# Stacked half blocks in neighbourhood attention, linear attention in smaller steps, and raw weight transfers issued later

## The chip, the cores and the metric

The kernel runs on one core of a Trainium2 chip. Its time is the device time of one execution, in microseconds. The core has TensorE (matrix products, written to eight PSUM banks), VectorE, ScalarE (ACT) and GpSimd (POOL) for the rest, and SyncE (SP), whose queue issues nearly all transfers. Every engine works through its own list of instructions in order, and they meet at semaphores.

## The reference, cut to what matters

One inference step of a two-layer model of width 2048, on 128 context tokens and 512 latent tokens (640 columns in all):

```
per layer:  h = rms_norm(x) * (1 + scale) + shift          # from a conditioning vector
            y = mixer(h @ w_in) * silu(gate);  x = x + g * (y @ w_out)
layer 1:    windowed attention (8 heads)  ||  gated linear attention (4 heads, both directions)
layer 2:    neighbourhood attention (8 heads)  ||  chunked spatial gating

gla_scan, per chunk:   att = tril(qi @ ki.T)
                       o   = att @ v + qi @ S
                       S   = exp(blast) * S + ks.T @ v

neighbourhood_attention: 64 columns x 8 rows of latent tokens; each query sees 8 rows x 16 columns
                       of keys near it and all 128 context keys; softmax; o = p @ v
```

All numbers are float32. Projections are done to nearly float32 precision with three fast products: a weight w is split into whi (rounded) and wlo (the remainder), an activation into acth and actl, and acth*whi + actl*whi + acth*wlo is summed.

## The kernel before, in words

**The stream of projections.** A chunk is 128 output columns of a projection. `units` goes through the 16 k-tiles of a chunk in quads and through two halves of 320 (or 322) tokens; each k-tile and half is three matmuls. Raw weights come into `wraws`, four buffers of 512 columns that rotate (`wslot`, `wneed`); ACT makes whi and POOL wlo (`wpump`), into rings with room for five quads (`whl`). A raw load goes out when the split that read its buffer is done.

**Other work between the projections.** Attention, linear attention and the modulation sums are Python generators (tasks). While the program is written, `Pace` keeps a clock for every engine, for SP and for the transfers, from cost formulas; `self.now` is TensorE's. After every few projection matmuls `tick` lets tasks write their next step, up to the next `yield`. `until(x)` yields until the planner believes x ready; `bank()` yields until the next small PSUM bank is believed free. So the planner decides only where an instruction stands in its engine's list; on the chip the engine then waits for what is not really there. `dma` puts a transfer into SP's list at once if its buffer is believed ready, else into `late`, from which `dmas` issues it when it is.

**Banks.** In the first layer three banks are for the projections (`npj` is 3) and three (`top` is 6) rotate for everything small (`sm`); two hold rows of the modulation. From the end of the first layer's attention `npj` is 5.

**Linear attention** (`gla_pe`, one run a head): transposes of the decayed keys `KS` of both directions, local products (`At`), states (`p`), then the outputs `outs` for chunks (0, 1), (2) and (3, 4), with a state update on VectorE (`next_state`) in between. State updates read the banks that `states` filled and write two buffers in turn, which `outs` reads. The values have been transposed just before by `tok_major` (four blocks in a bank, the fifth in the next).

**Windowed attention** (`even_head`): after the scores, one group of matmuls in one bank, with 512 columns for the context and then 256, 384, 384 and 256 for the four key blocks, all of 128 rows. `rope` first turns the queries, with four transfers within SBUF and work on VectorE and POOL.

**Neighbourhood attention** (`na_head`): keys are taken in five blocks, the first and the last of 64 tokens, the three between of 128. Values (`vk`) and probabilities (`pT`) are transposed block by block. The output group is one 512-column matmul for the context, one of 128 columns on 64 rows, three of 256 columns on 128 rows and one of 128 columns on 64 rows. `open_na` lays out the buffers.

In the profile L400 is the one line at which all matmuls are issued, L405 the one for transposes, L436 that for transfers, L215 that for everything on ACT, VectorE and POOL. "Y" and "arena" are large areas from which many buffers are cut.

## Time and profile before

| | us |
|---|---|
| median of 3 runs | 2090.88 (2089.56 to 2090.99) |
| the profiled execution's own time | 2094.82 |
| its span in the profile | 2093.0 |
| TensorE busy | 2047.3 |
| VectorE, POOL, ACT busy | 1327.3, 1275.1, 1064.4 |

In rows of the view in order of time, the first number is the start, the second how long the row's instructions take together, then engine, line, operation, what it writes and reads, shape, and how many (x); in brackets how long the engine was idle before, and who ended that. A row of waits has the total, the number and the longest. TensorE's ends are modelled, so the steady rate is read from starts. A plain float32 matmul leaves two records, a transpose one. In rows by stretch come the stretch, its length, busy time of TensorE, of weight loads, of VectorE, ACT and POOL with instruction counts, the granted clock, and the transfers' share and rate.

### The profile page before, as it was taken

To read this page: it belongs to the slowest core of one execution; us is meant where nothing else is said; L and a number is where in the kernel's file an instruction comes from. 1 tells how busy PE (TensorE), PEld (TensorE's weight loads), DVE (VectorE), ACT (ScalarE), POOL (GpSimd) and SP (SyncE) were. 2 spreads that over 40 slices of the span, in tenths; PEclk is the share of its full clock that TensorE was granted. 3 is DMA by queue.
4 is the path that set the end of the run, shared out by engine and by line. 5 is a ranking of instruction groups with operands and counts; after the bars stand their busy time and mean duration, and the time that the engine had idled before them with its cause. 6 is when DMAs were issued, how large, how long until landed. Compare 5 with 4: busy or idle time off the path is not lost. (4 is left out here: it accounts for less than half of the span.)

```text
span 2093.0 us, 40200 instructions
## 1 busy us (share of the span) xinstructions
PE 2047.3 (98%) x14345; PEld 1995.9 (95%) x14345; DVE 1327.3 (63%) x3070; ACT 1064.4 (51%) x2446; POOL 1275.1 (61%) x1072
## 2 busy tenths in 40 slices
PE   7999999999999999999999999999999999999997
PEld 6889999999999999999999999999999999999997
DVE  4757677676555655788786878787454554456444
ACT  5545555445665765444564434444444554454443
POOL 4655454445545554788765666655555577768884
PEclk9999999999999999999999999999999999999998
DMA  9956333436456444577734454454322334363427
GB/s 367 396 195 205 124 122 110 142 112 188 153 170 190 142 137 148 167 222 226 249 131 135 136 159 153 139 156 139 98 86 95 95 129 135 112 235 121 139 90 251
DMA packets 192697, 340.18 MB, mean 163 GB/s; under 512 B 20752, under 2 KB 70000, under 8 KB 192496
## 3 DMA queue, kind: packets, MB, share of 16 engines
q1 hardware_dynamic: 191296, 336.45, 49.7%
q8 instruction: 112, 1.84, 0.4%
q10 hardware_dynamic: 1200, 1.17, 0.2%
q14 instruction: 89, 0.73, 0.1%
HBM read 303.03 MB, written 31.88 MB: 160 GB/s over the span
## 5 line engine op out<-in xcount | busy, mean ns | idle before, releaser
L400 PE MATMUL bank<-acth,whi 128*128 128x320 f32 (+3 forms) x3320 | 1017.7, 317 | 4.7 <-ACT YB L215 1.4
L400 PE MATMUL bank<-acth,wlo 128*128 128x320 f32 (+3 forms) x3320 | 991.7, 310 | 0.9 <-POOL wlo L215 0.9
L400 PE MATMUL bank<-actl,whi 128*128 128x320 f32 (+3 forms) x3320 | 991.5, 310 | 0.0
L215 POOL TENSOR_TENSOR wlo<-wraw,whi 128x512 fp32r<-128x512 f32 (+1 forms) x446 | 568.1, 1285 | 439.1 <-ACT whi L215 368.4
L400 PEld LDWEIGHTS bank<-acth,whi 128*128 128x128 f32 (+1 forms) x3320 | 614.9, 188 | 12.5 <-issue 3.0
L400 PEld LDWEIGHTS bank<-actl,whi 128*128 128x128 f32 (+1 forms) x3320 | 615.5, 188 | 1.7
L400 PEld LDWEIGHTS bank<-acth,wlo 128*128 128x128 f32 (+1 forms) x3320 | 614.1, 188 | 1.9 <-POOL wlo L215 1.9
L215 POOL TENSOR_TENSOR wlo<-rs,whi 128x384 fp32r<-128x384 f32 x370 | 407.9, 1120 | 205.6 <-ACT whi L215 173.2
L215 ACT ACTIVATE whi<-wraw 128x512 fp32r<-128x512 f32 (+1 forms) x456 | 261.3, 588 | 126.7 <-PE bank L400 85.7
L215 ACT ACTIVATE whi<-rs 128x384 fp32r<-128x384 f32 x370 | 184.4, 518 | 83.2 <-PE bank L400 69.1
L400 PE MATMUL bank<-eh,whi 128*128 128x322 f32 (+1 forms) x666 | 208.9, 314 | 1.0 <-ACT whi L215 1.0
L400 PE MATMUL bank<-eh,wlo 128*128 128x322 f32 (+1 forms) x666 | 206.8, 310 | 1.2 <-POOL wlo L215 0.9
L400 PE MATMUL bank<-el,whi 128*128 128x322 f32 (+1 forms) x666 | 206.3, 310 | 0.0
L215 DVE CUSTOM_DVE_ANT_0 adas<-adas,bank,partg 128x256 bf16<-128x256 f32 (+1 forms) x296 | 160.6, 543 | 15.6 <-DMA adas<-ada_g 8.0
L215 DVE TENSOR_TENSOR wraw<-rs 128x768 f32<-128x768 f32 x74 | 98.8, 1335 | 100.7 <-DMA rs<-w_odd 55.4
L215 POOL TENSOR_TENSOR prod<-adas,mixrow 128x512 f32<-128x512 f32 x76 | 99.4, 1317 | 68.5 <-ACT prod L215 47.9
L215 ACT ACTIVATE arena<-arena,bc 128x512 f32<-128x512 f32 (+4 forms) x189 | 97.8, 538 | 78.6 <-DVE arena L215 73.7
L400 PEld LDWEIGHTS bank<-eh,wlo 128*128 128x128 f32 x666 | 125.1, 188 | 2.4 <-POOL wlo L215 2.4
L400 PEld LDWEIGHTS bank<-eh,whi 128*128 128x128 f32 x666 | 125.4, 188 | 1.3 <-ACT whi L215 1.2
L400 PEld LDWEIGHTS bank<-el,whi 128*128 128x128 f32 x666 | 125.4, 188 | 0.0
L215 DVE CUSTOM_DVE_ANT_0 adas<-adas,bank,part 128x512 bf16<-128x512 f32 x150 | 111.6, 744 | 19.6 <-DMA adas<-ada 16.7
L215 DVE TENSOR_TENSOR bank<-bank,sums 128x320 f32<-128x320 f32 (+1 forms) x148 | 70.8, 493 | 82.5 <-PE bank L400 61.3
(226 smaller groups left out, 2458.9 us busy)
## 6 DMA issues: line engine op xcount, KB each, us to landing
wraw<-w_even SPq DMA_DIRECT2D x176, 256.0 KB, 3.4
adas<-ada_g SPq DMA_DIRECT2D x128, 256.0 KB, 3.7
adas<-ada SPq DMA_DIRECT2D x128, 256.0 KB, 3.7
rs<-w_odd SPq DMA_DIRECT2D x50, 384.0 KB, 3.3
wraw<-w_odd SPq DMA_DIRECT2D x74, 256.0 KB, 3.6
wraw<-w_out SPq DMA_DIRECT2D x60, 256.0 KB, 3.9
rs<-w_odd SPq DMA_DIRECT2D x50, 256.0 KB, 3.8
Y<-ada SPq DMA_DIRECT2D x24, 512.0 KB, 7.8
```

Of the source, the lines that this page charges most:

```text
L215: return f(*args, **kw)
L400: self.nc.tensor.matmul(out, lhsT, rhs, start=start, stop=stop, **kw)
```

## The change

Four things are edited.

1. `dma`: while `npj` is 3, a transfer into `wraws` is put into SP's list 2.0 us of the planner's clock after its buffer is believed ready.
2. `gla_pe`: the transposes of the keys are written in three steps instead of two (four of one direction, the two last blocks, four of the other); steps wait with `bank()` for a free bank, and some start 0.5 or 0.6 us later.
3. `na_head`: the first and last 64-token blocks share one 128-row block. In `vk` the last block's values go to rows 64 to 127 beside the first block's in rows 0 to 63. In `pT` the two have their own 128 columns and zeros in the other 64 rows (two memsets in `open_na`). One matmul with 256 moving columns then writes the first and the fourth quarter of the bank. The last block is transposed with the 64 tokens before it, so that it comes out in rows 64 to 127.
4. `na_head`: where two probability blocks lie side by side, one copy of 256 columns takes the place of two.

```
-        if pc.ready("q", o, i) <= self.now + 0.1:
+        lag = 2.0 if self.npj == 3 and out.name.rstrip("0123456789_").startswith("wraw") else 0.0
+        if pc.ready("q", o, i) + lag <= self.now + 0.1:
             emit()
         else:
-            pc.late.append((emit, o + i, lambda: pc.ready("q", o, i)))
+            pc.late.append((emit, o + i, lambda: pc.ready("q", o, i) + lag))
...
-        yield from self.until(KS[0], KS[1])
-        pb = self.sm()
+        yield from self.until(KS[1])
+        yield 0.6
+        yield from self.bank()
         pa = self.sm()
         for i in range(4):
             self.tr(pa[:, c(i)], KS[1][:, c(i)])
+        nc.scalar.activation(KS[1][:, 0:512], pa, AF.Copy)
+        yield from self.until(KS[0])
+        yield 0.6
+        yield from self.bank()
+        pb = self.sm()
         self.tr(pb[:, 0:128], KS[1][:, c(4)])
         self.tr(pb[:, 128:256], KS[0][:, c(4)])
-        nc.scalar.activation(KS[1][:, 0:512], pa, AF.Copy)
         nc.scalar.activation(KS[1][:, 512:640], pb[:, 0:128], AF.Copy)
         nc.scalar.activation(KS[0][:, 512:640], pb[:, 128:256], AF.Copy)
-        yield
+        yield 0.6
+        yield from self.bank()
...
         yield from self.until(At, Sb)
+        yield 0.5
+        yield from self.bank()
         outs((0, 1), (None, S))
         S3 = next_state(S2, 2)
         yield from self.until(S2)
+        yield from self.bank()
         outs((2,), (S2,))
         S4 = next_state(S3, 3)
         yield from self.until(S4)
+        yield 0.5
+        yield from self.bank()
         outs((3, 4), (S3, S4))
...
-        for i, t in ((0, 0), (1, 4)):
-            a, e = edges[t]
-            self.tr(pv[:64, 128 * i : 128 * i + 128], vl[:, a:e])
-        nc.scalar.activation(vk[:64, 512:768], pv[:64, 0:256], AF.Copy)
+        self.tr(pv[:64, 0:128], vl[:, 0:64])
+        self.tr(pv[:, 128:256], vl[:, 384:512])
+        nc.scalar.activation(vk[:64, 512:640], pv[:64, 0:128], AF.Copy)
+        nc.scalar.activation(vk[64:, 512:640], pv[64:, 128:256], AF.Copy)
...
+            if b in (1, 2):
+                s = slot[(b, b)]
+                nc.vector.tensor_copy(pT[:, s : s + 256], pt[:, 128:384])
...
-        self.mm(po[:, 0:128], vkt[0], pT[:64, 768:896], start=False, stop=False)
         for j in (1, 2, 3):
...
-        self.mm(po[:, 384:512], vkt[4], pT[:64, 896:1024], start=False, stop=True)
+        ends = po.rearrange("p (a b) -> p a b", b=128)[:, 0:4:3, :]
+        self.mm(ends, vk[:, 512:640], pT[:, 768:1024].rearrange("p (a b) -> p a b", b=128), start=False, stop=True)
...
+            nc.gpsimd.memset(L["pT"][64:, 768:896], 0.0)
+            nc.gpsimd.memset(L["pT"][:64, 896:1024], 0.0)
```

What this does to the order of instructions is shown at three places. First, TensorE at the key transposes of the linear attention's first head. Banks 68 and 69 are projections, 70 to 72 the three small ones; "ident" marks a transpose, the arena holds the values and one direction's keys, Y the other's. Before:

```order
L400 MATMUL bank_69<-acth,wlo 128x320
L405 MATMUL bank_71<-ident,arena_1639 128x128 x4
L405 MATMUL bank_72<-ident,arena_1639 128x128
L405 MATMUL bank_71<-ident,arena_1639 128x128 x4
L405 MATMUL bank_70<-ident,arena_1639 128x128
L405 MATMUL bank_70<-ident,Y 128x128
```

and now:

```order
L405 MATMUL bank_71<-ident,arena_1639 128x128 x4
L405 MATMUL bank_72<-ident,arena_1639 128x128
L400 MATMUL bank_69<-acth,whi 128x320
L400 MATMUL bank_69<-actl,whi 128x320
L400 MATMUL bank_69<-acth,wlo 128x320
...
L405 MATMUL bank_70<-ident,arena_1639 128x128 x4
...
L405 MATMUL bank_71<-ident,arena_1639 128x128
L405 MATMUL bank_71<-ident,Y 128x128
```

The values' transposes (the first two rows of transposes) were followed at once by the keys', back into bank 71. Now six projection matmuls stand between, the keys' four go to bank 70, and after six more the last two go to bank 71.

Second, TensorE at the same head's outputs. Before:

```order
L400 MATMUL bank_71<-Y,arena_1639 128x128 x8
L400 MATMUL bank_72<-Y,arena_1639 128x128 x6
L400 MATMUL bank_69<-acth,whi 128x320
L400 MATMUL bank_69<-actl,whi 128x320
L400 MATMUL bank_69<-acth,wlo 128x320
...
L400 MATMUL bank_70<-Y,arena_1639 128x128 x12
```

and now:

```order
L400 MATMUL bank_71<-Y,arena_1639 128x128 x8
L400 MATMUL bank_69<-acth,whi 128x320
L400 MATMUL bank_69<-actl,whi 128x320
L400 MATMUL bank_69<-acth,wlo 128x320
...
L400 MATMUL bank_72<-Y,arena_1639 128x128 x6
L400 MATMUL bank_67<-acth,whi 128x322
L400 MATMUL bank_67<-actl,whi 128x322
L400 MATMUL bank_67<-acth,wlo 128x322
...
L400 MATMUL bank_70<-Y,arena_1639 128x128 x12
```

The outputs of chunks 0 and 1 (x8) and of chunk 2 (x6) stood together; now six projection matmuls lie between them, and twelve, where there were six, before the last (x12).

Third, SP's list ahead of the first query head's rotary transfers in windowed attention ("Y<-arena", four transfers of 32 rows). Before:

```order
L436 DMA adas<-ada 128x512 x3
L436 DMA wraw<-w_even 128x512
L436 DMA adas<-ada 128x512 x2
L436 DMA Y<-arena_4740 32x512 x3
L436 DMA adas<-ada 128x512
L436 DMA Y<-arena_4740 32x512
```

and now:

```order
L436 DMA adas<-ada 128x512
L436 DMA wraw<-w_even 128x512
L436 DMA adas<-ada 128x512 x3
L436 DMA wraw<-w_even 128x512
L436 DMA Y<-arena_4744 32x512 x3
L436 DMA adas<-ada 128x512
L436 DMA Y<-arena_4744 32x512
```

Raw loads ("wraw") stand further back among the modulation loads ("adas"); here one has come to stand directly ahead of the rotary transfers.

## The prediction

> **What bounds the kernel now.** I read the page's busy times first, then busy time by stretches, then TensorE's own waits stage by stage, and last the order in time at the places that the change touches.

> ```profile
> span 2093.0 us, 40200 instructions
> PE 2047.3 (98%) x14345; PEld 1995.9 (95%) x14345; DVE 1327.3 (63%) x3070; ACT 1064.4 (51%) x2446; POOL 1275.1 (61%) x1072
> 200.00:300.00 100.00, 97.19 (x663) 94.62 (x662) 75.36 (x131) 54.77 (x109) 48.34 (x33) 1.00 0.38 116
> 1550.00:1650.00 100.00, 100.00 (x669) 96.76 (x668) 43.09 (x114) 47.85 (x119) 57.41 (x53) 1.00 0.31 99
> ```

> TensorE (first number after the stretch's length) is busy for 98% of the span, and no other engine comes near. What counts is therefore only what TensorE does and what makes it stand still. The linear attention of the first layer (200 to 470 us) leaves it idle for some us; the neighbourhood attention of the second layer (1350 to 1700 us) leaves it nothing, so there only shorter matrix work can help. The granted clock is 1.00 in both rows.

> The waits of TensorE, first from 145 to 840 us, then from 215 to 470 us alone:

> ```profile
> PE bank L405 <- ACT arena L215: 5.2, 8, 1.8
> PE bank L400 <- DVE arena L215: 4.0, 5, 2.2
> PE bank L405 <- DVE sh L215: 1.1, 1, 1.1
> PE bank L400 <- ACT bc L215: 0.6, 1, 0.6
> ...
> PE bank L405 <- ACT arena L215: 3.1, 6, 0.6
> PE bank L400 <- DVE arena L215: 1.8, 4, 0.8
> ```

> Ten waits lie in the linear attention, 4.9 us as the view counts them. No row names whi or wlo, the split weights: from 145 to 840 us TensorE never stood waiting for a weight.

> **Linear attention, the transposes.** The last of the four heads on TensorE, and ACT beside it:

> ```profile
> 444.43 0.32 PE L400 MATMUL bank<-acth,wlo 128*128 128x322 f32 x1
> 444.58 0.71 PE L405 MATMUL bank<-ident,arena 128*128 128x128 f32 x5
> 445.87 0.77 PE L405 MATMUL bank<-ident,arena 128*128 128x128 f32 x5 [0.58 <-ACT arena L215]
> ...
> 445.22 0.77 ACT L215 ACTIVATE arena<-bank 128x512 f32<-128x512 f32 x2 [0.47 <-PE bank L405]
> ```

> The row ahead is the last projection matmul: what follows it starts 0.15 us later, and so does each projection in a run of them. Five transposes of the values are followed at once by five of the keys. The first four of both go to the same bank (the order shown with the change has it), so the second group waits until ACT has copied that bank out, from 445.22 on. A transpose in an unbroken row takes 0.108 us (worked out below). Five are 0.54, and the next group starts after 445.87 - 444.58 = 1.29, not 0.54. The view's 0.58 starts only at the modelled end of the last transpose, which overlaps the next start when nothing waits, so the path loses the whole difference, 0.75. Taken for the four heads this is 4 x 0.75 = 3.0 us. The change puts the keys' four in the third bank, six projection matmuls later. What hides the copy is then 6 x 0.15 = 0.9 us of projections. Without them, the third bank would still be free of that copy.

> **Linear attention, the outputs.** Heads one and four on TensorE, then VectorE in head four:

> ```profile
> 236.97 1.95 PE L400 MATMUL bank<-Y,arena 128*128 128x128 f32 x16
> 239.70 1.60 PE L400 MATMUL bank<-Y,arena 128*128 128x128 f32 x12 [0.78 <-DVE arena L215]
> ...
> 458.90 1.95 PE L400 MATMUL bank<-Y,arena 128*128 128x128 f32 x16
> 461.20 1.60 PE L400 MATMUL bank<-Y,arena 128*128 128x128 f32 x12 [0.35 <-DVE arena L215]
> ...
> 460.67 0.48 DVE L215 SCALAR_TENSOR_TENSOR arena<-arena,etot,bank 128x256 f32<-128x256 f32 x1 [2.16 <-PE bank L400]
> ```

> Here TensorE hands to VectorE and back: the state update at 460.67 waits for the first outputs and takes 0.48, and the next outputs wait for it. Sixteen records at 0.112 take 1.79 us; the next group starts after 2.30 in head four and after 2.73 in head one. That loses 0.51 and 0.94, and the other two heads show 0.35 like head four. Together 0.94 + 3 x 0.51 = 2.5 us. The change asks for a free bank before the second group, and at least six projections (0.9 us) come between. They cover 0.51 entirely and 0.94 nearly; if VectorE is busy with something else, up to the old 2.5 us comes back.

> Do more and smaller pieces cost anything by themselves? Four transposes between projections:

> ```profile
> 225.52 0.60 PE L405 MATMUL bank<-ident,Y 128*128 128x128 f32 x4
> 225.87 0.39 PE L400 MATMUL bank<-acth,whi 128*128 128x322 f32 x1
> 226.10 0.31 PE L400 MATMUL bank<-actl,whi 128*128 128x322 f32 x1
> ```

> From 225.52 to the second projection, 0.58; less one projection (0.15) that is 0.43, four transposes at 0.108. Changing over costs nothing that can be seen, so three more pieces a head are free. Of 3.0 + 2.5 I take off 0.1 for head one, whose 0.94 is more than the cover, and put **-5.4 us** on the linear attention. Its bounds are 0, if each wait comes back elsewhere, and -6.3 us, if the two waits that are left (3.1 us of ACT waits in six rows, less 4 x 0.58, is 0.8) go too.

> **Half blocks.** A head's last group of matmuls in neighbourhood attention, with the first projections behind it; then the same kind of group in the first layer's windowed attention, where every block has 128 rows; then durations by form, and the weight loads of the first group:

> ```profile
> 1357.03 3.34 PE L400 MATMUL bank<-Y 128*128 128x512 f32 x12
> 1360.30 0.41 PE L400 MATMUL bank<-acth,whi 128*128 128x320 f32 x1
> 1360.55 0.31 PE L400 MATMUL bank<-actl,whi 128*128 128x320 f32 x1
> ...
> 806.08 3.17 PE L400 MATMUL bank<-arena 128*128 128x512 f32 x10
> 808.90 0.50 PE L400 MATMUL bank<-acth,whi 128*128 128x320 f32 x1
> 809.24 0.31 PE L400 MATMUL bank<-actl,whi 128*128 128x320 f32 x1
> ...
> L400 PE MATMUL bank<-Y 64*128 64x128 f32 x32 | 7.8, 322 | 0.0
> L400 PE MATMUL bank<-Y 128*128 128x128 f32 x16 | 3.1, 275 | 0.0
> ...
> 1357.98 1.58 PEld L400 LDWEIGHTS bank<-Y 64*128 64x128 f32 x8 [0.76 <-issue]
> ```

> Each plain f32 matmul leaves two records. The windowed group has 512 + 256 + 384 + 384 + 256 = 1792 columns, 3584 in its ten records; from 806.08 to 809.24 less one projection of 0.15 is 3.01 us, 0.84 ns a column. The neighbourhood group has 512 + 128 + 3 x 256 + 128 = 1536 columns, 3072 in twelve records: at 0.84 they should take 2.58. They take 1360.55 - 1357.03 - 0.15 = 3.37. The 0.79 too much belongs to the two half blocks: their weight loads start only after the matmuls before them are through (0.76 of idle ahead of the first), where full blocks load behind running matmuls, and each of their records is longer than a full one of the same width (322 against 275 ns). The change has the same 1536 columns with 128 rows everywhere, so 2.58 us a head. TensorE is never idle in that stage, nothing else can take the place of the bound, and 8 x 0.79 = **-6.3 us** follow.

> [...]

> What no row shows is a matmul that writes two separate quarters of a bank. It lies between a full 256-column matmul (2 x 0.216 at 0.84 ns a column) and the pair it replaces (that plus 0.79). I take the first, because nothing but the view of the bank differs.

> The rest of this edit is off the path. VectorE has two copies fewer a head (two of 128 columns become one of 256, twice), ACT one more of 64 rows by 128 columns. Transposing 128 instead of 64 columns does not show in these rows, nor does the memset, twice 64x128 once:

> ```profile
> L405 PE MATMUL bank<-ident,Y 128*128 128x128 f32 x82 | 15.9, 273 | 0.0
> L405 PE MATMUL bank<-ident,Y 128*64 128x128 f32 x15 | 4.1, 272 | 0.0
> L215 ACT ACTIVATE Y<-bank 64x256 f32<-64x256 f32 x7 | 2.6, 367 | 0.0
> L215 POOL MEMSET part<- 128x64 f32 x1 | 0.2, 151 | 0.0
> ```

> ACT gains below 0.37 us a head at 48% busy; POOL gets at most 2 x 0.2 us, with weight remainders behind it. Uncovered, either would be under 3 us.

> **The held transfers.** A raw load now goes out 2.0 us (by the planner's clock) after its buffer is free, behind the modulation loads issued meanwhile. Transfers to landing, POOL's splits and the SP queue's waits:

> ```profile
> wraw<-w_even SPq DMA_DIRECT2D x176, 256.0 KB, 3.4
> L215 POOL TENSOR_TENSOR wlo<-wraw,whi x155: 1007/1293/2446, 144.3 to 833.6; 128x512 fp32r<-128x512 f32 x154, 128x384 fp32r<-128x384 f32 x1
> SPq L436 <- POOL wlo L215: 204.5, 92, 9.0
> ```

> 155 splits in 689 us are one in 4.4 us, and four buffers rotate, so a buffer is read again about 17.8 us after its last split. Less 1.3 for the split and 3.4 for landing, about 13 us are spare; 2.0 of them cost nothing. SP stood 204.5 us for POOL between 145 and 640 us; some of that goes, and what is queued behind (modulation, state and rotary transfers) may start earlier. TensorE waited for none of them but one:

> ```profile
> 543.16 1.83 DVE L215 TENSOR_TENSOR arena<-arena 128x512 f32<-128x512 f32 x1 [4.48 <-DMA Y<-arena]
> 546.71 0.49 PE L400 MATMUL bank<-arena 128*128 128x128 f32 x2 [2.15 <-DVE arena L215]
> ```

> This is windowed attention's first head, waiting for the rotary step on VectorE, which had waited for its transfers. In the new order its scores stand six projections earlier (138 instead of 144 behind the value head's transposes), while the query's own place is the same. So this wait should grow by 6 x 0.15: **+0.9 us**, between -2.2 (wait gone) and +3 (a raw load now stands directly ahead of the rotary transfers).

> **The sum.** -5.4 - 6.3 + 0.9 = -10.8 us on the profiled execution's own 2094.8 us, 2084.0. That execution stands 3.9 us above the median of 2090.88, so the median should come to **2080.1 us**.

> **The rivals.**
> (a) The hold frees the SP queue more than I count: the rotary wait (2.15) and the two left-over ACT waits (0.8) go. Then 2080.1 - 0.9 - 2.2 - 0.8 = 2076.2. For it: 204.5 us of SP waiting. Against: most of what SP carries is not waited for by TensorE.
> (b) The linear attention's waits only move, to the next bank or the next state: 2080.1 + 5.4 = 2085.5. For it: three banks in rotation and VectorE 70% busy there. Against: 0.9 us of projections at each place.
> (c) Row count does not matter and the half blocks give nothing: 2080.1 + 6.3 = 2086.4. Against: 0.79 us of surplus beside a group of full blocks.
> (d) Slower: the hold reaches the path at the four raw buffers. It decides once bursts of splits eat the 13 us; each load that misses its turn costs TensorE up to 2.0 us. One load in ten of the 155, 15 or 16, would be 31 us, 2111; it takes eight for 2096. Against: not one wait for a weight before.

> **How the numbers follow.** My forecast 0.57, (a) 0.14, (b) 0.17, (c) 0.04, (d) 0.03, and 0.05 for changes of order in windowed attention that I cannot price. What this kernel's measurement can tell from no change is 0.2%, 4.2 us, so below 2086.7 is faster. The first three cases are 0.88, with half of (c) and a little of the rest: 0.91 faster, 0.06 same, 0.03 slower. The range runs from 2075.0, a little under (a), to 2086.0, a little over (b).

> **What would show it.** In the changed profile no record of a 64-row matmul, the neighbourhood group at 2.6 us instead of 3.4, no 0.58 wait for ACT among the keys' transposes, no wait for VectorE between the outputs, still no wait for whi or wlo, and about 3 us at the first rotary wait. I am wrong if the neighbourhood group stays over 3 us, if a new row of waits of a few us stands in the linear attention, or if whi or wlo shows up among TensorE's waits before 840 us.

## The result, and the profile after

| | before | changed |
|---|---|---|
| median of 12 runs | 2090.03 us | 2084.37 us |
| lowest and highest | 2086.29 and 2097.17 | 2080.28 and 2089.64 |
| the profiled execution's own time | 2094.82 | 2084.71 |

The ratio is 0.9969, with a 95% interval of 0.9959 to 0.9978: the change makes the kernel about 6 us faster. The forecast was 2080.1 us, 10.8 less than before. The sign came as forecast and the time lies inside the range (2075.0 to 2086.0), but little more than half of the gain arrived. The profiled executions lie 10.1 us apart, which looks like the forecast's sum. It isn't: the one of before stood 4.8 us over the median of its kernel, the one of the change 0.3. So what follows reads pieces out of the profiles, and takes totals from repeated runs.

The page of the changed kernel, its first lines:

```profile
span 2082.9 us, 40154 instructions
PE 2042.3 (98%) x14329; PEld 1999.2 (96%) x14329; DVE 1329.2 (64%) x3048; ACT 1070.5 (51%) x2460; POOL 1276.9 (61%) x1077
```

TensorE is the bound as before. In neighbourhood attention, the last matmul group of a head and the projections behind it, in order of time:

```profile
1352.43 2.75 PE L400 MATMUL bank<-Y 128*128 128x512 f32 x10
1354.83 0.50 PE L400 MATMUL bank<-acth,whi 128*128 128x320 f32 x1
1355.16 0.31 PE L400 MATMUL bank<-actl,whi 128*128 128x320 f32 x1
```

From 1352.43 to 1355.16, less one projection of 0.15, is 2.58 us: what the prediction gave for 1536 columns at 0.84 ns, to the hundredth. The groups by form, from 1300 to 1760 us, of the changed kernel (busy time, mean ns of one, idle time before):

```profile
L400 PE MATMUL bank<-Y 128*128 128x256 f32 x64 | 15.1, 379 | 0.0
L400 PEld LDWEIGHTS bank<-Y 128*128 128x128 f32 x88 | 15.9, 190 | 5.1 <-issue 3.8
```

and of the kernel before, where the records of 64 rows stood beside those of 128:

```profile
L400 PE MATMUL bank<-Y 128*128 128x256 f32 x48 | 12.5, 396 | 0.0
L400 PEld LDWEIGHTS bank<-Y 128*128 128x128 f32 x72 | 12.2, 189 | 1.8
L400 PEld LDWEIGHTS bank<-Y 64*128 64x128 f32 x32 | 4.7, 184 | 8.7 <-issue 7.4 <-DVE partg L215 0.7 <-DVE arena L215 0.3
```

The form with 64 rows is gone, and with it the 8.7 us of idle time ahead of its weight loads. The loads of 128 rows now stand idle for 5.1 us instead of 1.8, so of 10.5 us in all, 5.4 are saved. The 16 new records (two for each of eight heads) that write two separate quarters of a bank are among the 64, and these take 379 ns on average, not more than the 396 of the 48 before; the group as a whole runs at the 0.84 ns a column of a group without such a view. So the strided output shows no cost.

In the linear attention, TensorE's waits from 215 to 470 us, and then the fourth head's value and key transposes and its first two output groups:

```profile
PE bank L400 <- DVE Y L215: 0.9, 1, 0.9
PE bank L400 <- ACT bc L215: 0.7, 1, 0.7
PE bank L405 <- ACT arena L215: 0.7, 2, 0.4
```

```profile
441.24 0.71 PE L405 MATMUL bank<-ident,arena 128*128 128x128 f32 x5
442.67 0.60 PE L405 MATMUL bank<-ident,arena 128*128 128x128 f32 x4
...
457.40 1.95 PE L400 MATMUL bank<-Y,arena 128*128 128x128 f32 x16
460.07 1.50 PE L400 MATMUL bank<-Y,arena 128*128 128x128 f32 x12
```

The 0.58 ahead of the key transposes and the 0.35 ahead of the second outputs (445.87 and 461.20 before) are gone: projections stand in between now, and neither row has a wait. Of the ten old waits, 4.9 us, two are left with 0.7 us. But two new ones have come that the kernel before had nowhere in this stretch:

```profile
294.25 0.41 PE L400 MATMUL bank<-acth,whi 128*128 128x320 f32 x1 [0.75 <-ACT bc L215]
...
342.81 0.41 PE L400 MATMUL bank<-r,wgs 96*128 96x320 f32 x1 [0.92 <-DVE Y L215]
```

By who ends these waits, both are for work that ACT and VectorE have not finished yet. Together they take 1.67 us.

Then comes windowed attention. In order of time around 510 us, VectorE, ACT and TensorE, and the place at 845 us:

```profile
505.63 3.48 DVE L215 TENSOR_TENSOR Y<-Y,arena 128x512 f32<-128x512 f32 x2 [2.44 <-DMA arena<-Y]
509.03 0.73 DVE L215 CUSTOM_DVE_ANT_0 adas<-adas,bank,partg 128x512 bf16<-128x512 f32 x1
...
512.98 0.75 DVE L215 CUSTOM_DVE_ANT_0 adas<-adas,bank,partg 128x512 bf16<-128x512 f32 x1
513.65 0.49 DVE L215 TENSOR_TENSOR arena<-bank,rstd 128x320 f32<-128x320 f32 x1
514.17 0.17 ACT L215 ACTIVATE bc<-bank 128x2 f32<-128x2 f32 x1 [2.63 <-DVE arena L215]
514.39 0.41 PE L400 MATMUL bank<-acth,whi 128*128 128x320 f32 x1 [2.08 <-ACT bc L215]
...
844.91 0.72 PE L400 MATMUL bank<-acth,whi 128*128 128x320 f32 x2 [1.96 <-ACT eh L215]
```

This is read backwards. TensorE waits for ACT, ACT for VectorE's copy at 513.65, and VectorE works in order: ahead of that copy stand six modulation sums (adas), ahead of them the rotary step of a key head, and that had waited 2.44 us for its transfers within SBUF. The same place before, with five sums between the first two rows:

```profile
509.69 3.47 DVE L215 TENSOR_TENSOR Y<-Y,arena 128x512 f32<-128x512 f32 x2 [3.09 <-DMA adas<-ada_g]
...
516.91 0.49 DVE L215 TENSOR_TENSOR arena<-bank,rstd 128x320 f32<-128x320 f32 x1
...
517.65 0.41 PE L400 MATMUL bank<-acth,whi 128*128 128x320 f32 x1 [0.55 <-ACT bc L215]
```

There the rotary step had waited no less (3.09 us), and TensorE stood for 0.55 us only. Counted from the start of the rotary step, VectorE's copy now begins after 8.02 us instead of 7.22, and TensorE's wait after 6.68 instead of 7.41; these two make up the 1.53 us by which the wait has grown. By stretches:

```profile
200.00:300.00 100.00, 98.42 (x677) 96.08 (x675) 79.53 (x133) 55.35 (x110) 50.20 (x34) 1.00 0.38 119
...
500.00:600.00 100.00, 95.62 (x618) 91.40 (x617) 58.19 (x160) 58.76 (x162) 54.03 (x41) 0.97 0.52 170
515.05:521.88 6.83, 6.14 (x25) 5.68 (x24) 4.93 (x13) 5.76 (x14) 4.88 (x5) 0.50 0.76 243
800.00:900.00 100.00, 97.23 (x638) 95.19 (x637) 70.23 (x139) 48.53 (x103) 67.42 (x52) 0.98 0.56 178
```

The granted clock, the third number from the end, is 1.00 in the linear attention. After the wait of 2.08 us it is 0.50 for 6.83 us, after that of 1.96 for 3.41 us. Projections then start 0.268 us apart instead of 0.147, so 3.41 us at 0.50 lose about 1.5 us. The kernel before had 0.50 nowhere between 100 and 2060 us of its profile.

The raw loads, waits of SP's queue from 145 to 640 us, in the changed kernel:

```profile
SPq L436 <- POOL wlo L215: 156.7, 66, 9.8
```

It was 204.5 us in 92 waits. And from 145 to 840 us no wait of TensorE names whi or wlo.

### The profile page after: what moved, and what is told of

Same layout as the page of the kernel before. It is cut to its first block, busy times and chain, and to the rows that moved or that the text cites. A ratio compares the mean times of both kernels' runs of the same rounds, so it can differ in the third digit from the quotient of the medians.

```text
span 2082.9 us, 40154 instructions
## 1 busy us (share of the span) xinstructions
PE 2042.3 (98%) x14329; PEld 1999.2 (96%) x14329; DVE 1329.2 (64%) x3048; ACT 1070.5 (51%) x2460; POOL 1276.9 (61%) x1077
## 5 line engine op out<-in xcount | busy, mean ns | idle before, releaser
L400 PE MATMUL bank<-acth,whi 128*128 128x320 f32 (+3 forms) x3320 | 1021.5, 319 | 8.6 <-ACT bc L215 2.8
L400 PE MATMUL bank<-acth,wlo 128*128 128x320 f32 (+3 forms) x3320 | 993.2, 310 | 0.9 <-POOL wlo L215 0.8
L400 PE MATMUL bank<-actl,whi 128*128 128x320 f32 (+3 forms) x3320 | 993.3, 310 | 0.0
L215 POOL TENSOR_TENSOR wlo<-wraw,whi 128x512 fp32r<-128x512 f32 (+1 forms) x446 | 566.1, 1282 | 450.9 <-ACT whi L215 374.0
L400 PEld LDWEIGHTS bank<-acth,whi 128*128 128x128 f32 (+1 forms) x3320 | 616.4, 188 | 16.8 <-ACT bc L215 4.8
L400 PEld LDWEIGHTS bank<-actl,whi 128*128 128x128 f32 (+1 forms) x3320 | 617.1, 189 | 1.9
L400 PEld LDWEIGHTS bank<-acth,wlo 128*128 128x128 f32 (+1 forms) x3320 | 615.8, 188 | 1.5 <-POOL wlo L215 1.4
L215 POOL TENSOR_TENSOR wlo<-rs,whi 128x384 fp32r<-128x384 f32 x370 | 406.3, 1117 | 189.5 <-ACT whi L215 156.0
L215 ACT ACTIVATE whi<-wraw 128x512 fp32r<-128x512 f32 (+1 forms) x456 | 261.6, 589 | 126.3 <-PE bank L400 82.9
L215 ACT ACTIVATE whi<-rs 128x384 fp32r<-128x384 f32 x370 | 184.2, 519 | 77.3 <-PE bank L400 62.3
L400 PE MATMUL bank<-eh,whi 128*128 128x322 f32 (+1 forms) x666 | 208.7, 313 | 0.0
L400 PE MATMUL bank<-eh,wlo 128*128 128x322 f32 (+1 forms) x666 | 206.4, 310 | 0.2 <-POOL wlo L215 0.2
L400 PE MATMUL bank<-el,whi 128*128 128x322 f32 (+1 forms) x666 | 206.3, 310 | 0.0
L215 DVE CUSTOM_DVE_ANT_0 adas<-adas,bank,partg 128x256 bf16<-128x256 f32 (+1 forms) x296 | 160.8, 543 | 14.0 <-DMA adas<-ada_g 5.4
L215 DVE TENSOR_TENSOR wraw<-rs 128x768 f32<-128x768 f32 x74 | 96.8, 1308 | 97.9 <-DMA rs<-w_odd 40.9
L215 POOL TENSOR_TENSOR prod<-adas,mixrow 128x512 f32<-128x512 f32 x79 | 101.8, 1299 | 62.2 <-ACT prod L215 49.4
L215 ACT ACTIVATE arena<-arena,bc 128x512 f32<-128x512 f32 (+4 forms) x189 | 98.0, 540 | 74.3 <-DVE arena L215 69.4
L400 PEld LDWEIGHTS bank<-eh,wlo 128*128 128x128 f32 x666 | 125.1, 188 | 0.5 <-POOL wlo L215 0.5
L400 PEld LDWEIGHTS bank<-eh,whi 128*128 128x128 f32 x666 | 125.4, 188 | 0.1
L400 PEld LDWEIGHTS bank<-el,whi 128*128 128x128 f32 x666 | 125.3, 188 | 0.0
L215 DVE TENSOR_TENSOR bank<-bank,sums 128x320 f32<-128x320 f32 (+1 forms) x148 | 70.7, 493 | 84.2 <-PE bank L400 63.1
L215 DVE CUSTOM_DVE_ANT_0 adas<-adas,bank,part 128x512 bf16<-128x512 f32 x147 | 109.4, 744 | 16.4 <-DMA adas<-ada 13.6
## 6 DMA issues: line engine op xcount, KB each, us to landing
wraw<-w_even SPq DMA_DIRECT2D x176, 256.0 KB, 3.7
adas<-ada_g SPq DMA_DIRECT2D x128, 256.0 KB, 3.6
adas<-ada SPq DMA_DIRECT2D x128, 256.0 KB, 3.6
wraw<-w_odd SPq DMA_DIRECT2D x74, 256.0 KB, 3.6
wraw<-w_out SPq DMA_DIRECT2D x60, 256.0 KB, 3.8
rs<-w_odd SPq DMA_DIRECT2D x50, 256.0 KB, 3.9
```

The lines of the kernel that those rows point to most:

```text
L215: return f(*args, **kw)
L400: self.nc.tensor.matmul(out, lhsT, rhs, start=start, stop=stop, **kw)
```

## The experiments

The theory was: each part does in its place about what the prediction's rows say, and part of it is lost later, where a wait of nearly 2 us in windowed attention or at the handover behind it lowers the clock. Its rivals: one part is simply worth less than forecast; the hold costs more than its 0.9 us; the lowered clock belongs to something else than waits.

### Each part alone, and the change without the hold

First the half blocks and the joint copies alone (edits 3 and 4):

```
-        self.mm(po[:, 0:128], vkt[0], pT[:64, 768:896], start=False, stop=False)
...
-        self.mm(po[:, 384:512], vkt[4], pT[:64, 896:1024], start=False, stop=True)
+        ends = po.rearrange("p (a b) -> p a b", b=128)[:, 0:4:3, :]
+        self.mm(ends, vk[:, 512:640], pT[:, 768:1024].rearrange("p (a b) -> p a b", b=128), start=False, stop=True)
...
```

> Only the stacked half blocks (edits 3 and 4), the rest as before. Theory A (my sum: half blocks -6.3, linear attention -5.4, hold +0.9): -6.3 us, ratio 0.9970, with the neighbourhood group at 2.6 us in all eight heads and nothing else moved ahead of 1300 us. Theory B (the half blocks carry the whole measured gain of some 6 us, the other edits cancel): also -6 us. Theory C (row count does not matter): 0.

Then the linear attention's steps alone (edit 2):

```
+        yield 0.6
+        yield from self.bank()
         pa = self.sm()
         for i in range(4):
             self.tr(pa[:, c(i)], KS[1][:, c(i)])
...
```

> Only the linear attention's smaller steps (edit 2). Theory A: -5.4 us, ratio 0.9974, no wait of 0.58 for ACT and none of 0.35 to 0.78 for VectorE between 215 and 470 us. Theory B: the waits named are gone, but others of the same size come back behind them (in the next chunk's evacuation, or at the windowed attention), and the time is within 1.5 us of before.

The hold alone (edit 1):

```
-        if pc.ready("q", o, i) <= self.now + 0.1:
+        lag = 2.0 if self.npj == 3 and out.name.rstrip("0123456789_").startswith("wraw") else 0.0
+        if pc.ready("q", o, i) + lag <= self.now + 0.1:
...
```

> Only the held raw transfers (edit 1). Theory A: +0.9 us (first scores six projections earlier, the wait at the first rotary step near 3 us), no wait for whi or wlo before 840 us, SP's waiting for POOL well under 204 us between 145 and 640 us. Theory B: the hold costs more, +2 to +5 us, through a wait near 2 us or more at the windowed attention after which the granted clock drops to 0.5 for some us. Theory D: waits for whi or wlo, over +5 us.

And everything but the hold:

```
-        lag = 2.0 if self.npj == 3 and out.name.rstrip("0123456789_").startswith("wraw") else 0.0
-        if pc.ready("q", o, i) + lag <= self.now + 0.1:
+        if pc.ready("q", o, i) <= self.now + 0.1:
...
```

> The changed kernel without the hold (edits 2, 3 and 4). Theory A: 6.3 + 5.4 = -11.7 us, 0.9944. Theory B, if it is the hold that gives back: -9 to -11 us; if the linear attention's own waits come back: -6 us, as the whole change.

The whole change once more:

> The changed kernel once more, for a second profile of it. Theory B (the linear attention's gain is lost again in windowed attention): -6 us as measured, the linear attention (projections 1000 to 2500) 3.5 to 4 us shorter than before, and a wait of about 2 us at the chunk behind the first key head's rotary step near 514 us, with or without the granted clock at 0.5 behind it. Theory A': the 2.1 us wait and the slow clock of the first profile were chance, and the time is -9 us or better.

Measured, each against runs of the kernel before on the same chip (the difference is that of the means, with its standard error):

| | median us | ratio, 95% interval | difference us |
|---|---|---|---|
| half blocks alone | 2083.50 | 0.9968, 0.9957 to 0.9979 | -6.75 +- 0.72 |
| linear attention alone | 2087.23 | 0.9985, 0.9976 to 0.9994 | -3.37 +- 0.63 |
| hold alone | 2090.81 | 1.0005, 0.9996 to 1.0014 | +0.87 +- 0.68 |
| all but the hold | 2083.33 | 0.9969, 0.9956 to 0.9981 | -6.70 +- 0.55 |
| whole change again | 2084.65 | 0.9975, 0.9966 to 0.9984 | -5.06 +- 0.78 |

Alone, the three parts are worth -6.75, -3.37 and +0.87, in sum -9.25 +- 1.5 (the three share their runs of before), close to the prediction's -10.8. Together they give -5.1 to -6.0. So the parts come near to what they should and don't add up. This is clearest without the hold: half blocks and linear attention, alone -10.1 in sum, give -6.70 together, 3.4 +- 1.0 less. Where this happens the following table shows. It takes the starts of six projection matmuls, the same in every kernel (number 1000, 2500, 4200, 5200, 7300 and 9800 of the 12102, at 211, 502, 825, 978, 1303 and 1739 us of the profile before), and gives by how much a stage between two of them is longer than in the profile of before, in us. The last column counts the stretches of 3.41 us at a granted clock of 0.50 between 100 and 2060 us.

```
                      linear     windowed   handover  next    neighbourhood  stretches
                      attention  attention            stage   attention      at 0.50
changed               -3.83      +2.28      -1.37     -0.29   -5.93          3
changed, again        -3.91      -1.36      -1.47     +0.45   -5.21          1
half blocks alone     -0.01      -1.81      -0.99     -0.95   -5.24          2
linear alone          -3.95      +1.31      -3.82     -0.53   +0.01          0
hold alone            -0.11      -2.22      -0.85     -0.69   +0.54          1
all but the hold      -3.86      +3.77      -1.27     -0.73   -5.48          2
```

The linear attention gives -3.83 to -3.95 in every kernel that has its steps, and nothing in the others; neighbourhood attention -5.2 to -5.9 likewise. These two are firm. In windowed attention and at the handover the columns jump by several us, also between two executions of one kernel. The half blocks alone have up to there TensorE's very order of instructions of before, and yet -1.81 in windowed attention: the profile of before had chance waits there (the 2.15 us at the first head's rotary step above all), so about 2 us of every negative number in that column is no gain. At the handover the kernel that gains 3.82 has no stretch at 0.50, and the five profiles that gain about 1 have one each. Against that base the changed kernel loses 4 us in windowed attention in its first profile, and half a microsecond in its second.

The wait at the end of windowed attention, first in the changed kernel's second profile, then in that of all but the hold:

```profile
841.73 0.72 PE L400 MATMUL bank<-acth,whi 128*128 128x320 f32 x2 [1.92 <-ACT eh L215]
```

```profile
841.51 0.88 PE L400 MATMUL bank<-acth,whi 128*128 128x320 f32 x2 [1.98 <-ACT eh L215]
```

and of the latter the stretch around it:

```profile
840.00:850.00 10.00, 8.49 (x46) 8.38 (x47) 9.99 (x19) 6.80 (x14) 10.00 (x7) 0.83 0.18 60
```

Before it was 1.31 without a change of clock. With the changed order it is 1.96 and 1.92 here, and 1.87, 1.77 and 2.11 in the three kernels with gaps below, which have the same order up to neighbourhood attention; five times of five a stretch at 0.50 follows. The wait at 514 us comes and goes: 2.08 with two stretches in the first profile, 1.63 without any in the second. Ahead of neighbourhood attention these five profiles have 3, 1, 1, 2 and 3 stretches, 2.0 on average; the two with before's order there (before, half blocks alone) have 0 and 2. And the order without the hold has 2 in one profile (all but the hold) and none in the other (linear alone, the same order up to there). So the changed order seems to fall into the lowered clock more often, but five profiles against two do not say how much.

A stretch at 0.50 does not need one long wait. The half blocks alone have two shorter ones close together at the handover, and then the lowered clock:

```profile
881.66 0.41 PE L400 MATMUL bank<-eh,whi 128*128 128x320 f32 x1 [0.96 <-ACT whi L215]
...
882.74 0.42 PE L400 MATMUL bank<-eh,wlo 128*128 128x320 f32 x1 [0.53 <-POOL wlo L215]
```

```profile
883.91:887.32 3.41, 3.41 (x14) 3.16 (x14) 2.83 (x7) 0.45 (x2) 2.72 (x3) 0.50 0.00 0
```

The hold alone has the same pair (0.98 and 0.52) and a stretch at 0.50 behind it. The kernel before has it too (0.95 and 0.52), without one.

The hold explains little of it: alone it costs 0.87, and without it the change gains 0.7 to 1.6 us more, within the errors. It moves the waits, though: the one at 514 us, 1.63 to 2.19, stands in all five profiles of the changed order, and in none without the hold; these two have one at the first head's rotary step instead (1.10 and 1.99 at 537 us). What the hold does to SP's queue, in the run with the hold alone:

```profile
SPq L436 <- POOL wlo L215: 159.5, 62, 9.0
```

### Is it the wait that lowers the clock?

Gaps were put into neighbourhood attention, where TensorE hardly waits by itself (0.2 us in all from 1300 to 1760 us of the changed kernel). They are added work and leave the outputs as they are: a transpose into a small bank, k copies of that bank onto itself by ACT, another transpose that must wait for them. With one gap a head and six copies, eight long gaps; with three gaps a head and two copies, 24 short ones; with three and one copy, 24 shorter ones.

```
+    def gap(self, k):
+        yield from self.bank()
+        p = self.sm()
+        self.tr(p[:, 0:128], self.ident)
+        for _ in range(k):
+            self.nc.scalar.activation(p, p, AF.Copy)
+        self.tr(p[:, 0:128], self.ident)
+        yield 1.0
...
+        yield from self.gap(6)
```

> The changed kernel with eight deliberate waits of TensorE in neighbourhood attention, one a head: a transpose, six copies of a bank by ACT onto itself, a transpose into it (nothing of the output depends on them). Each wait should be 3.3 to 3.8 us. Theory K (a stretch of 3.4 us in which TensorE stands for about 1.9 us or more is followed by one at half clock): 8 to 13 steps of 3.41 us at 0.5 in the granted clock, and 14 to 22 us lost beyond the waits themselves. Theory L (only the wait costs): no step at 0.5 there, nothing lost beyond the waits.

> The same with 24 waits of 1.2 to 1.5 us (two copies each, three a head), about the same idle time in all. Theory K: no step at 0.5, or one or two where ACT is late, and under 4 us lost beyond the waits. Theory L: as above, nothing lost beyond the waits, so that both kernels lose the same for each us of idle time.

> Added work only, outputs unchanged: the 24 gaps of the run before, each with one copy by ACT instead of two. The wait a copy adds is about 0.7 us there (4.65 us with six copies, 1.9 with two), so each gap should be about 1.2 us. If a lowered clock needs close to 2 us of standing within one stretch of 3.41 us, no stretch at 0.5 should appear between 1300 and 1760 us (at most one or two where two gaps fall close together), and the time is 2084.5 + 24 x 1.2 + about 24 x 0.4 of ends and transposes = 2123. If the clock follows the sum of the idle time instead (about 29 us here, beside 37 us with eight long gaps, which had 44 us at 0.5), about 34 us at 0.5 appear and the time is 17 us more, 2140.

TensorE's waits from 1300 to 1760 us, and then one stretch of 100 us. With the eight long gaps:

```profile
PE bank L405 <- ACT bank L215: 37.2, 8, 5.3
```

```profile
1400.00:1500.00 100.00, 91.34 (x585) 88.96 (x585) 69.38 (x219) 49.90 (x125) 50.37 (x46) 0.95 0.35 112
```

With the 24 short ones, the same two views:

```profile
PE bank L405 <- ACT bank L215: 45.2, 24, 2.5
```

```profile
1400.00:1500.00 100.00, 88.69 (x571) 85.42 (x570) 63.59 (x198) 46.85 (x116) 48.99 (x46) 0.97 0.34 111
```

And with the 24 shorter ones:

```profile
PE bank L405 <- ACT bank L215: 30.8, 24, 1.9
```

```profile
1400.00:1500.00 100.00, 91.59 (x611) 87.96 (x610) 65.18 (x210) 47.41 (x122) 50.26 (x48) 1.00 0.34 108
```

The eight long gaps brought 13 stretches at 0.50 into this stage (44.4 us; 8 to 13 were expected), the 24 short ones ten (34.1), the 24 shorter ones a single one. The second kernel was meant as the control without any, but its gaps came out at 1.9 us on average instead of 1.2 to 1.5, so it missed; the third was made for that. It stands still for 30.8 us in all, not much less than the 37.2 of the first, and keeps a clock of 1.00. The sum of idle time over the stage does not matter then; what falls close together does, be it one wait near 2 us or, as above, two shorter ones (the last section has the step within which they count). The third kernel's only stretch at 0.50 comes behind its longest wait of this stage but one. TensorE there in order of time, and the clock by stretches:

```profile
1369.47 0.27 PE L405 MATMUL bank<-ident 128*128 128x128 f32 x1
1371.65 0.33 PE L405 MATMUL bank<-ident 128*128 128x128 f32 x1 [1.91 <-ACT bank L215]
1371.74 0.39 PE L400 MATMUL bank<-acth,whi 128*128 128x322 f32 x1
...
1378.55 0.33 PE L405 MATMUL bank<-ident 128*128 128x128 f32 x1 [1.55 <-ACT bank L215]
```

```profile
1372.70:1376.10 3.40, 3.40 (x16) 3.32 (x15) 2.61 (x4) 0.70 (x2) 0.43 (x1) 0.50 0.91 319
1376.10:1400.00 23.90, 22.35 (x155) 21.91 (x155) 18.24 (x68) 12.16 (x34) 11.63 (x11) 1.00 0.37 119
```

1.91 us is followed by 0.50 within about a microsecond, 1.55 by nothing. The three kernels took 2145.64, 2154.69 and 2126.43 us in one run each. A gap costs its wait and about 0.36 for the two transposes (1369.47 to 1371.74 is 2.27 for a wait of 1.91). For the last that makes 30.8 + 24 x 0.36 + 1.5 for the one stretch, 40.9 over the change's 2084.5, or 2125.4; for the 24 short gaps 45.2 + 8.6 + 10 x 1.5, 2153.3. For the eight long gaps the same sum gives 37.2 + 2.9 + 13 x 1.5 = 59.6, or 2144.1. All three are about 1.5 us or less from what was measured, in one execution each. The profiles show the stage by itself: in the last two kernels it is 42.2 and 69.5 us longer than in the change, near the 40.9 and 68.8 of the sum, so the lowered clock has its price right. With the long gaps it is 56.5 us longer, not 59.6, because part of the half clock lies within the waits themselves (in the one of 5.28 us that ends at 1378.35 it has begun before 1376.10); that the total agrees there is chance. The expected 2123 for the last rested on waits of 1.2 instead of 1.3 us.

### Taking the wait away

The key head's rotary step was waiting for transfers within SBUF that the planner believes landed 1.0 us after their end. Here it believes 3.0, and so puts what needs them later. Nothing else is edited, and the hold stays:

```
+            inside = bass.MemoryType.DRAM not in (out.space, in_.space)
-            pc.note("q", o, i, pc.t["d"] + (self.ROWS if rows else 1.0))
+            pc.note("q", o, i, pc.t["d"] + (self.ROWS if rows else 3.0 if inside else 1.0))
```

> The changed kernel, with transfers within SBUF believed to land 2 us later, so that VectorE's rotary work stands three modulation sums further back in its list and the next chunk's evacuation only three sums behind it instead of six. Theory B (what the linear attention gained is lost at the rotary steps, by VectorE's in-order wait for those transfers and by the clock behind TensorE's wait): no wait over 1 us between 500 and 560 us, no half clock there, and 3 to 5 us faster than the whole change, -9 to -11 us against before. Theory A (losses are spread over the windowed attention): as the whole change, within 1.5 us.

Then the same without the hold, and the same with the half blocks alone (before's linear attention and raw loads):

> The change without the held transfers, with the planner believing that transfers within SBUF land 3.0 instead of 1.0 us after their end. If the three effects add up (linear attention -3.9 in place, neighbourhood attention -5.2 to -5.9, no wait near 2 us in windowed attention, no hold), -9 to -10 us against before: about 2080.5, and 1 to 3 us below the change. If the transfers' landing has nothing to do with the loss, it comes out like the change without the hold: -6.7, about 2083.5.

> The half blocks alone with the later landing of transfers within SBUF; linear attention and raw loads as before. If the later landing gives something by itself, -6.7 (half blocks alone) and 1 to 2 us more, about 2082; if it only repairs what the new order of the linear attention had brought about, -6.7, about 2083.5. Against the kernel with the linear attention's steps as well it should be 3 to 4 us slower if these add up, and equal if they are lost again.

> The same kernel as in the run of the rotary step without the hold, a second time: its five times were 2076.3 to 2078.4. If that is what the order of its instructions brings (no wait near 2 us in windowed attention and at the handover, so no stretch at half clock), it comes again between 2076 and 2079, about 13 us under the kernel before, with no row of the clock under 1.00 between 100 and 2060 us. If the five were a lucky draw, its times spread over 2076 to 2085 like those of the other kernels here, and stretches at 0.5 appear.

| | median us | lowest to highest | ratio, 95% interval | difference us |
|---|---|---|---|---|
| later landing, with hold | 2081.66 | 2077.88 to 2090.34 | 0.9966, 0.9955 to 0.9978 | -6.99 +- 1.2 |
| later landing, no hold | 2076.43 | 2076.26 to 2078.43 | 0.9938, 0.9926 to 0.9951 | -13.2 +- 0.7 |
| the same again | 2077.67 | 2076.33 to 2080.11 | 0.9927, 0.9910 to 0.9944 | -14.7 +- 1.2 |
| later landing, half blocks alone | 2087.40 | 2084.26 to 2091.33 | 0.9988, 0.9978 to 0.9997 | -2.38 +- 0.9 |

```
                             linear     windowed   handover  next    neighbourhood  stretches
                             attention  attention            stage   attention      at 0.50
later landing, with hold     -3.90      -3.17      -0.78     -0.91   -4.81          2
later landing, no hold       -4.01      -1.72      -3.87     -0.91   -6.11          0
the same again               -3.95      -1.36      -3.70     -0.91   -5.13          0
later, half blocks alone     -0.08      -0.68      +3.98     +0.09   -5.05          2
```

The second and third line are one kernel, and it beats both the kernel before (by 13 to 15 us) and the change. It was expected at 2080.5, from the parts in place, and came 3 to 4 us under that. Against all but the hold, from which it differs by that one figure, it is 6.5 to 8 us faster (both measured against before). TensorE at the two places in its second profile, in order of time, and then the clock by stretches:

```profile
515.59 0.66 PE L405 MATMUL bank<-ident,arena 128*128 128x128 f32 x4 [1.08 <-ACT arena L215]
...
839.39 0.72 PE L400 MATMUL bank<-acth,whi 128*128 128x320 f32 x2 [1.55 <-ACT eh L215]
```

```profile
500.00:600.00 100.00, 98.22 (x662) 94.85 (x661) 55.35 (x161) 63.52 (x173) 54.78 (x42) 1.00 0.55 176
...
800.00:900.00 100.00, 98.12 (x656) 96.52 (x655) 70.39 (x145) 49.59 (x105) 66.40 (x54) 1.00 0.59 184
```

Between 100 and 2060 us no wait reaches 1.6 us, no 3.41 us hold that much idle time together, and no stretch at 0.50 appears, in either profile of it. The gains of the two parts arrive here in full, and windowed attention and handover give nothing back; the handover even gains 3.7 to 3.9 where the orders with a stretch at 0.50 there gain 1, as the linear attention's steps alone also did.

The later landing is not good by itself, though. With the half blocks alone it was expected at or under 2083.5, and gave 2087.40, 4 us worse than the half blocks without it. Its profile shows more waits for weights at the handover than any other, 5.4 us in six (before 2.7 in five, the change 0.8 in one), and two stretches at 0.50, one of them right behind the longest of these waits. Two of them in order of time:

```profile
883.06 0.41 PE L400 MATMUL bank<-eh,whi 128*128 128x320 f32 x1 [1.21 <-ACT whi L215]
...
964.86 0.48 PE L400 MATMUL bank<-eh,wlo 128*128 128x320 f32 x1 [1.74 <-POOL wlo L215]
```

and by stretches:

```profile
900.00:1000.00 100.00, 98.06 (x653) 97.04 (x653) 84.03 (x189) 41.10 (x90) 85.34 (x79) 0.98 0.67 219
```

And with the hold it gave -7.0, 6 to 8 less than without, though the hold alone costs 0.9. The one profile of that kernel has no wait near 2 us in windowed attention (the theory's point), but a wait of 3.58 us with a stretch at 0.50 at 1886 us, far behind everything that was edited, and one more stretch, at 879 us, behind the pair of waits for weights (1.20 and 0.53). Its runs spread from 2077.88 to 2090.34. The wait of 3.58 us stands in one other profile, that of the eight long gaps, whose landing times are those of the change; so it does not belong to this edit. What releases it was not found, and why the hold takes so much away here is open.

## Why the prediction was right, and where it was not

**Half blocks, -6.3: right.** 2.58 us a head as computed, 0.79 saved, no record of 64 rows, no long wait in its place; alone -6.75 +- 0.72, in place -4.8 to -6.1 in the eight profiles that have them (waits of 0.2 to 1.1 us in all, which the profile of before does not have there, make most of the difference to 6.3). Rival (c) falls, and what it supposes of the row count no run shows: for two matmuls of 64 rows among ones of 128, each pair lost 0.79 us here. With the form of 64 rows the idle time ahead of the weight loads fell by 5.4 us, 0.68 a head. How much of the 0.79 is in those late loads and how much in the longer records (322 against 275 ns), no run here tells apart.

**Linear attention, -5.4: mechanism right, size off.** All waits that the term listed are gone, as its rows said. In place it measured -3.8 to -4.0. The difference of 1.5 is the two new waits at 294.25 and 342.81, 0.75 + 0.92 = 1.67; their rows (0.7 or 0.8, and 0.9) are the same in all ten profiles with this edit. The term took "three more pieces a head are free" from the cost of changing over between matmuls. It did not ask who empties the banks sooner: VectorE went from 75.36 to 79.53 us of 100 between 200 and 300 us, and TensorE now comes to the next places before VectorE and ACT are through. That the denser work of VectorE is the reason is argued from these figures, not tested. Rival (b) named this; 1.67 of 5.4, about a third of it, came true.

**The hold, +0.9: the number right by luck, the way not.** +0.87 +- 0.68 alone, which is not told apart from 0. SP's waits for POOL fell from 204.5 to 156.7 us, and no weight was waited for, so rival (d) falls. But the 3 us at the first head's rotary step did not come: in the changed profile that wait is gone, and the 2.15 us of before, on which the term was built, were chance. The half blocks alone, with the same order up to there, have no such wait. In its place, with the linear attention's steps beside the hold, came the 2.08 us at 514 us, an earlier point of the same stage.

**The sum, -10.8: the step that failed.** Two things stand between it and the -5.1 to -6.0 measured. The first is the 1.5 of the linear attention. The second has no term in the sum: the prediction read 1.00 for the granted clock in its two rows and took every wait at its own length, and it kept 0.05 of chance for "changes of order in windowed attention that I cannot price". There and at the handover the changed order has waits of 1.63 to 2.19 us, and two stretches at half clock on average behind them (five profiles), about 1.5 us each beside the waits, where before's order has one (two profiles). That the gaps bring the same (0.50 behind a wait of 1.91 us) shows that waits of this length can lower the clock; that the order with the later landing and no hold has neither and reaches -13 to -15 agrees with the loss lying there. Yet it is not settled how the 3 to 4 us divide: one stretch more is 1.5, the longer waits around 1 us, and the stage moves by 3.6 us between two executions of the changed kernel alone. Linear alone and all but the hold, -3.37 and -6.70, have the same order up to neighbourhood attention and should differ by the half blocks' 6.75, but do by 3.3. Their profiles show where: at the same places the one has waits of 1.10 and 0.97 us and no lowered clock, the other of 1.99 and 1.98 with a stretch at 0.50 behind each, 5.0 us longer in these two stages. One execution of each does not say why the second should be so more often; that is open.

**The base.** "That execution stands 3.9 us above the median of 2090.88, so the median should come to" 3.9 less: the step takes the excess for the same after. It was chance waits of one execution, some of which the terms counted as the kernel's own. The changed kernel's profile stood 0.3 over its median.

## What to carry to other kernels

Before pricing a wait that may grow or appear, look at what else stands idle within 3.41 us of it: in these profiles waits that together came to 1.90 us or more within one step cost themselves and then half speed for 3.41 us, and from 1.49 us on they did so in some executions. A step that makes one stage denser should be checked at the next readers of its banks, and the planner's beliefs on landing times checked against the trace before the order is tuned further, since one figure was worth as much here as the whole change, and was worth it only with the linear attention's steps and without the hold. Take the base of a sum from several executions, or at least ask of each wait in the one profile whether the order of instructions forces it.

## What had not been expected of the hardware

The grid does not stand at the same place in every execution. With multiples of 3.4133 us taken off the starts of the lowered clock, counted from the span's start, 3.02 us is left before (47.39), 3.05 in the changed kernel (515.05), 3.27 with the half blocks alone (883.91) and 0.54 with the 24 shorter gaps (1372.70). So the same wait may cost its length in one execution and more in the next, an estimated 1.5 to 3 us, from the 1.5 us that a stretch at 0.50 loses. That the two profiles of the changed kernel differ by two stretches at 514 us is not of this kind: both waits lay within one step, and 1.63 us was simply the shorter.
